# Layer 0's second and third late modulation burst: moved behind the scores of each half, their transposes laid out with the next burst's first step

## The chip, the cores and the metric

One core of one Trainium2 chip. The metric is the device time of one launch in microseconds (us). TensorE (PE) multiplies, VectorE (DVE), ScalarE (ACT) and GpSimd (POOL) work on SBUF and PSUM, and SyncE (SP) issues nearly all loads. Each engine works through its own list of instructions in order.

## The reference

Two layers (DEPTH 2) on one sequence, SEQ = D_MODEL = 1024, all in float32. What matters here, cut down:

```python
cond = jax.nn.silu(c)
for l in range(DEPTH):
    mod = (cond @ w_ada[l] + b_ada[l])[:, None, :]
    shift_a, scale_a, gate_a, shift_f, scale_f, gate_f = jnp.split(mod, N_MOD, axis=-1)
    h = rms_norm(x) * (1.0 + scale_a) + shift_a
    mix = hybrid_mixer(h, ...)          # gated linear attention (GLA) | latent attention (MLA)
    x = x + gate_a * mix
    h = rms_norm(x) * (1.0 + scale_f) + shift_f
    x = x + gate_f * (jnp.square(jax.nn.relu(h @ w_mlp_up[l])) @ w_mlp_down[l])
```

The six vectors of `mod` are numbered m = 0 to 5 in this order. So m = 2 (gate_a) is wanted after the mixer, and m = 3 and 4 (shift_f, scale_f) by the norm in front of the MLP. In the mixer, `h @ w_in` gives GLA's q, k (256 columns each), v, output gate g (512 each) and a decay input, and MLA's latents. GLA's scores inside a chunk are q k^T weighted with products of decays.

## The kernel before

**Matmuls.** A product is three fp32r matmuls on hi/lo splits of both operands (`mm3`: lines 161, 162, 163). A weight unit is loaded by SP (line 292, 512 KB), rounded to its high part on ACT or DVE (line 307) and its low part is the rest, made on POOL or DVE (line 308). 51 arena slots of 128x1024 hold all tiles; a slot that is freed is given to the next `AR.alloc()`, and its new load waits until the old tile's last reader is done. A name such as `s_141_1081` is slot counter and tile number.

**Order.** The list `PROGRAM` says in which order the mixer's code is written out; a scheduler then lays the instructions of all engines out by a simulated time line, with the order of the code as the priority. Halves A and B are the two halves of the 1024 tokens. The tokens that matter: `v` values and `g` gates of a half (weights as the moving operand, output token by token into four PSUM banks), `L` the latents with the decay input, `T` the rest of the latents (norms, decays `lg`, transposes), `Q` GLA's queries and keys, `W` GLA's scores, `O` GLA's output, `u` and `a` heads and attention of MLA, `H` the second half of the normed input.

**Scores (`gla_scores`, token W).** Score blocks are built level by level, H = 1, 2, 4, ..., 64, eight passes of score matmuls in all (line 912; one pass is eight instructions, which the profile counts as 16). For each level ACT makes exponentials of decays (lines 949, 955), DVE differences and sums of them (956, 961), POOL scales keys and queries (950, 927, 958), and the products come out of `ps_g` by DVE (938, 966, 973). Two tiles each for keys and queries alternate, which POOL clears first (902, 903). Then the keys are scaled and transposed (990, 998, 999), and `gla_out` multiplies (1038, 1042, 1048) and transposes its result (1068).

**Modulation bursts (`ada_steps`).** One vector m takes eight loads of 128x1024 of w_ada (line 245, 512 KB each), eight DVE steps that sum them with the condition as the scalar (line 254, then seven of line 256), eight PE transposes (line 263) and two DVE sums over the 128 partial columns (266, 267, and 269 for m = 1 and 4). In layer 0, m = 0 and 1 are made at the start, m = 2, 3, 4 by the tokens X2, X3, X4 in the mixer, m = 5 and layer 1's six vectors step by step inside the MLP of layer 0 (`ADA_ORDER`, `UP_ADA`, `DOWN_ADA`).

## Time and profile before

| | |
|---|---|
| time, three runs | 2334.77 us median (2326.91 to 2339.45) |
| the profiled execution | 2329.49 us, of it 2327.7 us span |
| PE busy | 2228.0 us, 96% of the span |
| DVE busy | 1785.4 us, 77% |
| ACT busy | 1137.8 us, 49% |
| POOL busy | 457.3 us, 20% |
| w_ada loads of 512 KB | 80, 5.1 us from issue to landing |

PE is at work nearly all the time, so what counts are the few places where it is not. The stages that the change touches lie between 50 and 365 us of the span. Busy time of matmuls is modelled at their ends, so starts are the better measure of PE's pace.

### The profile page before, as it was taken

The page shows a single profiled execution, that of the slowest core. Times are in us where ns is not written, and L with a number is a line of the kernel's source. Part 1 is how long each engine was busy: PE and PEld are TensorE (multiplying, and loading weights), DVE is VectorE, ACT ScalarE, POOL GpSimd, SP SyncE. Part 2 cuts the span into 40 slices and gives each one's busy share as a digit, 9 for nine tenths or more (in the row PEclk, how much of TensorE's full clock was granted, in tenths as well). Part 3 has the DMA queues.
Part 4 walks back from the last instruction along what each step waited for, and adds up shares of the span by engine and source line. Part 5 has one row for each costly group of instructions (what it writes and reads, how often), then busy time and mean ns, then how long its engine had stood idle before and what let it go on. Part 6 is the DMA issues. An engine that isn't in the chain of part 4 may idle for free.

```text
span 2327.7 us, 29242 instructions
## 1 busy us (share of the span) xinstructions
PE 2228.0 (96%) x11016; PEld 1851.0 (80%) x11016; DVE 1785.4 (77%) x2453; ACT 1137.8 (49%) x1764; POOL 457.3 (20%) x326
## 2 busy tenths in 40 slices
PE   7989999999999999998999999999999999999999
PEld 4778788888788877886888888887888888887887
DVE  5987769757989788889996756986665867887794
ACT  3464647535632483433535555665365228633341
POOL 2544533410030000000074345342002000000000
PEclk9999999999999999999999999999999999999999
DMA  9632210236678655765741221004354564365562
GB/s 345 202 105 81 82 30 1 82 106 221 207 220 276 192 163 200 243 229 193 241 138 34 63 61 41 10 10 125 130 160 138 184 196 145 113 231 195 166 208 82
DMA packets 236657, 340.41 MB, mean 146 GB/s; under 512 B 11078, under 2 KB 150500, under 8 KB 236516
## 3 DMA queue, kind: packets, MB, share of 16 engines
q1 hardware_dynamic: 235968, 338.08, 44.8%
q8 instruction: 86, 1.41, 0.3%
q14 instruction: 55, 0.45, 0.1%
q10 hardware_dynamic: 548, 0.48, 0.1%
HBM read 317.54 MB, written 20.97 MB: 145 GB/s over the span
## 4 chain that ended last, share of the span: by engine, by line
PE 66%; DVE 14%; DMA 7%; ACT 2%; issue 2%; POOL 1%; SPq 0%; DVEq 0%; ACTq 0%; POOLq 0%
PE ps_m L162 9%; PE ps_m L163 9%; PE ps_m L161 8%; PE ps_s L162 6%; PE ps_s L163 6%; PE ps_s L161 6%; PE ps_g L163 4%; PE ps_g L162 4%; PE ps_g L161 4%; DMA s<-in_w_mlp_down_dram 3%; PE ps_x L163 2%; PE ps_x L162 2%; DMA s<-in_w_ada_dram 2%; PE ps_x L161 2%; DMA s<-in_w_mlp_up_dram 2%
## 5 line engine op out<-in xcount | busy, mean ns | idle before, releaser
L307 ACT CAST s<-s 128x1024 fp32r<-128x1024 f32 (+2 forms) x306 | 314.8, 1035 | 474.1 <-DVE s L304 243.2
L162 PE MATMUL ps_m<-s,s 128*128 128x512 f32 (+2 forms) x1212 | 462.2, 382 | 15.4 <-DVE s L1273 15.4
L161 PE MATMUL ps_m<-s,s 128*128 128x512 f32 (+2 forms) x1212 | 460.4, 383 | 10.4 <-ACT s L1272 3.9
L163 PE MATMUL ps_m<-s,s 128*128 128x512 f32 (+2 forms) x1212 | 459.1, 379 | 1.6 <-DVE s L308 1.5
L308 POOL TENSOR_TENSOR s<-s,s 128x1024 fp32r<-128x1024 f32 (+2 forms) x90 | 229.2, 2558 | 1051.6 <-ACT s L307 696.5
L161 PE MATMUL ps_s<-s,s 128*128 128x512 f32 (+5 forms) x928 | 356.9, 388 | 9.0 <-ACT s L719 3.1
L163 PE MATMUL ps_s<-s,s 128*128 128x512 f32 (+5 forms) x928 | 354.6, 384 | 1.8 <-DVE s L308 1.3
L162 PE MATMUL ps_s<-s,s 128*128 128x512 f32 (+5 forms) x928 | 354.7, 383 | 0.0
L308 DVE TENSOR_TENSOR s<-s,s 128x1024 fp32r<-128x1024 f32 x224 | 270.0, 1217 | 55.8 <-ACT s L307 45.6
L304 DVE TENSOR_TENSOR s<-s,s 128x1024 f32<-128x1024 f32 x160 | 198.4, 1242 | 119.0 <-DMA s<-in_w_mlp_up_dram 81.7
L162 PEld LDWEIGHTS ps_m<-s,s 128*128 128x128 f32 x1212 | 230.4, 190 | 59.1 <-DVE s L1273 18.5
L161 PEld LDWEIGHTS ps_m<-s,s 128*128 128x128 f32 x1212 | 229.3, 189 | 54.9 <-ACT s L1272 6.1
L163 PEld LDWEIGHTS ps_m<-s,s 128*128 128x128 f32 x1212 | 230.0, 190 | 42.7 <-DVE s L308 2.5
L1272 ACT CAST s<-s 128x1024 fp32r<-128x1024 f32 x140 | 146.7, 1050 | 187.6 <-DVE s L1270 57.3
L161 PEld LDWEIGHTS ps_s<-s,s 128*128 128x128 f32 x928 | 174.7, 188 | 47.2 <-ACT s L719 6.1
L163 PEld LDWEIGHTS ps_s<-s,s 128*128 128x128 f32 x928 | 175.2, 189 | 37.8 <-issue 3.0
L162 PEld LDWEIGHTS ps_s<-s,s 128*128 128x128 f32 x928 | 175.4, 189 | 32.8 <-issue 1.5
L162 PE MATMUL ps_g<-s,s 128*128 128x512 f32 (+1 forms) x506 | 195.2, 387 | 0.7 <-DVE s L1273 0.7
L161 PE MATMUL ps_g<-s,s 128*128 128x512 f32 (+1 forms) x506 | 194.6, 388 | 0.0
L163 PE MATMUL ps_g<-s,s 128*128 128x512 f32 (+1 forms) x506 | 194.4, 387 | 0.1
L1273 DVE TENSOR_TENSOR s<-s,s 128x1024 fp32r<-128x1024 f32 x140 | 173.6, 1244 | 14.9 <-ACT s L1272 11.1
L162 PE MATMUL ps_x<-s,s 128*128 128x512 f32 (+3 forms) x362 | 124.2, 344 | 1.5 <-DVE s L743 1.5
(320 smaller groups left out, 3636.1 us busy)
## 6 DMA issues: line engine op xcount, KB each, us to landing
s<-in_w_mlp_up_dram SPq DMA_DIRECT2D x192, 512.0 KB, 4.8
s<-in_w_mlp_down_dram SPq DMA_DIRECT2D x192, 512.0 KB, 4.3
s<-in_w_ada_dram SPq DMA_DIRECT2D x80, 512.0 KB, 5.1
s<-in_w_in_dram SPq DMA_DIRECT2D x48, 512.0 KB, 3.8
s<-in_w_ada_dram SPq DMA_DIRECT2D x32, 256.0 KB, 4.1
xd<-s SPq DMA_DIRECT2D x16, 512.0 KB, 4.5
s<-in_w_out_dram SPq DMA_DIRECT2D x16, 512.0 KB, 4.3
s<-xd SPq DMA_DIRECT2D x16, 512.0 KB, 3.4
```

Source lines behind the costliest of these rows:

```text
L161: PE.matmul(o, lh, rh, start=start, stop=False)
L162: PE.matmul(o, lh, rl, start=False, stop=False)
L163: PE.matmul(o, ll, rh, start=False, stop=stop)
L304: V.tensor_tensor(raw[:, :n], raw[:, :n], u.second[:, :n], op=ALU.add if u.sign > 0 else ALU.subtract)
L307: (V.tensor_copy if u.eng[-2] == "v" else S.copy)(R(u.hi[:, :n]), raw[:, :n])
L308: (V if u.eng[-1] == "v" else G).tensor_tensor(R(u.lo[:, :n]), raw[:, :n], u.hi[:, :n], op=ALU.subtract)
L1272: S.copy(R(hi), t)
L1273: V.tensor_tensor(R(lo), t, hi, op=ALU.subtract)
```

## The change

In `PROGRAM`, X (m = 2) stays; the burst of m = 3 moves from ahead of `Hb WA` (scores of half A) to behind `TB`, ahead of `QB`; the burst of m = 4 moves from between `QB` and `WB` to behind `gB`, ahead of the first head. A burst is now taken from one generator for all three vectors, eight steps at a time: the eight loads and DVE steps are laid out by X, and the eight transposes and sums by the first step of the next X, and for the last vector by the new token Z behind `vB`. The bursts of the MLP hand their transposes on in the same way, and `DOWN_ADA` takes one step more at m = 2. Lines behind the edits have smaller numbers: 4 to 6 less up to line 590, 4 less from 591 to 1153 (L912 becomes L908, L961 L957, L256 L252).

```diff
--- before.py
+++ after.py
@@ -35,7 +35,7 @@
 
 
 PROGRAM = (
-    "vA E X2 R LA Ha =1 TA QA X3 Hb WA gA OA LB TB QB X4 WB gB u00 P1 vB u01 a00 P1 "
+    "vA E X R LA Ha =1 TA QA Hb WA gA OA LB TB X QB WB gB X u00 P1 vB Z u01 a00 P1 "
     "P1 a01 OB =2 F U1 a02 a03 a10 a12 a11 a13 U2 a20 a21 a22 U3 a23 M0 =3 a30 a31 F M1 a32 D0 D1 "
     "D2 =0 a33 F D3 D4 D5 F D6 D7 N "
 ).split()
@@ -57,7 +57,7 @@
 
 ADA_ORDER = ((0, 5), (1, 1), (1, 0), (1, 2), (1, 4), (1, 3), (1, 5))
 UP_ADA = {2: range(8), 4: range(8), 1: (2, 6), 7: (1, 3, 5, 7), 6: range(1, 7), 5: (1, 3, 5, 7), 3: range(1, 7)}
-DOWN_ADA = {m: range(1, 7) for m in (4, 5, 2)}
+DOWN_ADA = {4: range(1, 7), 5: range(1, 7), 2: range(7)}
 
 UP_ENGINES = {1: "vag"}
 TAGS = {
@@ -233,10 +233,6 @@
         k = l * 48 + m * 8 + d
         return mod[:, k:k + 1]
 
-    def ada(l, m):
-        for _ in ada_steps(l, m):
-            pass
-
     def ada_steps(l, m, tag=lambda: "x"):
         acc = AR.alloc()
 
@@ -255,8 +251,7 @@
             else:
                 V.scalar_tensor_tensor(acc, raw, cond[:, k:k + 1], acc, op0=ALU.mult, op1=ALU.add)
             AR.free(raw)
-            if k < 7:
-                yield
+            yield
         for hb in range(2):
             ps = bank(tag())
             for b in range(4):
@@ -268,7 +263,6 @@
             if m in (1, 4):
                 V.tensor_scalar(mod[:, k0:k0 + 4], mod[:, k0:k0 + 4], 1.0, None, op0=ALU.add)
         AR.free(acc)
-        yield
 
 
 
@@ -588,6 +582,8 @@
         G.tensor_tensor(m2[:, :, 32:64], src[:, :, 0:32], Sn[:, :, 32:64], op=ALU.mult)
         G.tensor_tensor(dst[:, :, 0, :], m1, m2, op=ALU.add)
         G.tensor_tensor(dst[:, :, 1, :], m1, m2, op=ALU.add)
+
+    ada_work0 = (None for m in (2, 3, 4) for _ in ada_steps(0, m))
 
 
     wg = cp.tile([32, 256], F32, name="wg")
@@ -1151,9 +1147,10 @@
                 flush()
             elif kind == "=":
                 tags = TAGS[rest]
-            elif kind == "X":
+            elif kind in "XZ":
                 if l == 0:
-                    ada(0, int(rest))
+                    for _ in range(8 if kind == "X" else 1):
+                        next(ada_work0, None)
             elif kind == "P":
                 ahead(ustate["pos"] + int(rest))
             elif kind == "D":
@@ -1323,7 +1320,7 @@
                     if left[b] == 0 and b != (0, 1):
                         square_relu(C[b][g])
                 if l == 0 and g in UP_ADA[m]:
-                    next(ada_work)
+                    next(ada_work, None)
             for hi, lo in moving:
                 AR.free(hi, lo)
             moving = moving_next
@@ -1390,7 +1387,7 @@
                 AR.free(hi, lo)
                 drop(u)
                 if l == 0 and g in DOWN_ADA.get(m, ()):
-                    next(ada_work)
+                    next(ada_work, None)
             for q in range(4):
                 for (r, c), sign in PRODUCTS[m][2]:
                     d = r * 4 + q
```

**PE, the end of the gates of half A.** The first fence is before, from the gates' last product on; in names such as `s19_159_1151` the first number is the slot, tiles 156 to 159 are the keys and queries of the levels, and a pass is two rows, one for each PSUM bank.

```order
L161 MATMUL ps_s_1336<-s15_168_1339,s32_74_410 128x512
L162 MATMUL ps_s_1336<-s16_169_1340,s32_74_410 128x512
L163 MATMUL ps_s_1336<-s15_168_1339,s32_74_410 128x512
L263 MATMUL ps_x_1106<-cs_81,s34_141_1081 128x128 x4
L263 MATMUL ps_x_1114<-cs_81,s34_141_1081 128x128 x4
L912 MATMUL ps_g_1177<-s19_159_1151,s47_156_1148 128x128 x4
L912 MATMUL ps_g_1183<-s19_159_1151,s47_156_1148 128x128 x4
L912 MATMUL ps_g_1197<-s18_158_1150,s24_157_1149 128x128 x4
L912 MATMUL ps_g_1203<-s18_158_1150,s24_157_1149 128x128 x4
```

Five more passes of two rows each follow there, and then the eight key transposes (L998). Now, from the gates' last product to the first output product (the levels' tiles are 147 to 150):

```order
L908 MATMUL ps_g_1180<-s40_149_1093,s33_148_1092 128x128 x4
L908 MATMUL ps_g_1186<-s40_149_1093,s33_148_1092 128x128 x4
L163 MATMUL ps_s_1279<-s16_159_1282,s32_74_410 128x512
L908 MATMUL ps_g_1200<-s9_150_1094,s41_147_1091 128x128 x4
L908 MATMUL ps_g_1206<-s9_150_1094,s41_147_1091 128x128 x4
L908 MATMUL ps_g_1220<-s40_149_1093,s33_148_1092 128x128 x4
L908 MATMUL ps_g_1226<-s40_149_1093,s33_148_1092 128x128 x4
L908 MATMUL ps_g_1240<-s9_150_1094,s41_147_1091 128x128 x4
L908 MATMUL ps_g_1246<-s9_150_1094,s41_147_1091 128x128 x4
L994 MATMUL ps_g_1262<-cs_81,s28_128_936 128x128 x4
L994 MATMUL ps_g_1268<-cs_81,s28_128_936 128x128 x4
L1038 MATMUL ps_g_1430<-s44_80_428,s50_145_1089 128x128 x4
```

Seven score passes stood behind the gates, with the transposes of m = 3 ahead of them; now three do, five stand among the gates' products, the transposes are gone, and output products have come forward.

**DVE, ahead of the scores of half A.** Before, behind the latents' norm (L961 and L956 are the first decay steps, on the tile `s_119`):

```order
L451 SCALAR_TENSOR_TENSOR s_124_931<-ps_x,colsv,s_124_931 128x512
L872 TENSOR_TENSOR s_126_948<-ps_x,s_126_948 128x512
L254 TENSOR_SCALAR s_141_1081<-s_142_1082,cond 128x1024
L256 SCALAR_TENSOR_TENSOR s_141_1081<-s_143_1084,cond,s_141_1081 128x1024
L256 SCALAR_TENSOR_TENSOR s_141_1081<-s_144_1087,cond,s_141_1081 128x1024
L256 SCALAR_TENSOR_TENSOR s_141_1081<-s_145_1090,cond,s_141_1081 128x1024
L256 SCALAR_TENSOR_TENSOR s_141_1081<-s_146_1093,cond,s_141_1081 128x1024
L256 SCALAR_TENSOR_TENSOR s_141_1081<-s_147_1096,cond,s_141_1081 128x1024
L961 TENSOR_TENSOR s_119_866<-s_119_866 128x512
L256 SCALAR_TENSOR_TENSOR s_141_1081<-s_148_1099,cond,s_141_1081 128x1024
L956 TENSOR_TENSOR s_161_1156<-s_119_866 128x512
L961 TENSOR_TENSOR s_119_866<-s_119_866 128x256x2
L256 SCALAR_TENSOR_TENSOR s_141_1081<-s_149_1102,cond,s_141_1081 128x1024
```

Now, from the line that makes the decays (L828, before L832) on:

```order
L828 SCALAR_TENSOR_TENSOR s_119_850<-ps_x,tmp 128x512 x2
L424 SCALAR_TENSOR_TENSOR tmp<-s_13_160,mod,s_4_123 128x512
L424 SCALAR_TENSOR_TENSOR tmp<-s_14_167,mod,s_4_123 128x512
L424 SCALAR_TENSOR_TENSOR tmp<-s_15_174,mod,s_4_123 128x512
L957 TENSOR_TENSOR s_119_850<-s_119_850 128x512
L952 TENSOR_TENSOR s_152_1099<-s_119_850 128x512
L445 SCALAR_TENSOR_TENSOR s_122_899<-ps_x,colsv,s_122_899 128x512
L957 TENSOR_TENSOR s_119_850<-s_119_850 128x256x2
L424 SCALAR_TENSOR_TENSOR tmp<-s_16_181,mod,s_4_123 128x512
L445 SCALAR_TENSOR_TENSOR s_123_907<-ps_x,colsv,s_123_907 128x512
L957 TENSOR_TENSOR s_119_850<-s_119_850 128x128x4
L426 SCALAR_TENSOR_TENSOR s_144_1080<-tmp,mod,s_144_1080 128x512
```

The eight steps of the burst are gone from here, and the first decay step stands ahead of the latents' norm (L445, before L451).

**DVE, behind the scores of half B.** Before, from the copies of the transposed keys (L999) to the first head's norm factors (L396); L645 empties a value bank:

```order
L999 COPY s_236_2190<-ps_g 128x512 x2
L655 TENSOR_REDUCE ssq<-s_253_2388 128x4
L645 TENSOR_TENSOR s_254_2389<-ps_s,s_254_2389 128x256
L645 TENSOR_TENSOR s_254_2389<-ps_x,s_254_2389 128x256
L651 TENSOR_REDUCE ssq<-s_255_2411 128x4
L652 TENSOR_REDUCE ssq<-s_255_2411 128x4
L391 TENSOR_SCALAR rs_v<-ssq 128x8
L391 TENSOR_SCALAR rs_v<-ssq 128x4
L394 SCALAR_TENSOR_TENSOR rs_a<-rs_y 128x12
L395 TENSOR_TENSOR rs_a<-rs_a,rs_v 128x12
L396 SCALAR_TENSOR_TENSOR rst<-rs_a,rs_y 128x12
```

Now:

```order
L995 COPY s_227_2131<-ps_g 128x512
L250 TENSOR_SCALAR s_242_2315<-s_243_2316,cond 128x1024
L995 COPY s_227_2131<-ps_g 128x512
L252 SCALAR_TENSOR_TENSOR s_242_2315<-s_244_2318,cond,s_242_2315 128x1024
L252 SCALAR_TENSOR_TENSOR s_242_2315<-s_245_2321,cond,s_242_2315 128x1024
L641 TENSOR_TENSOR s_254_2371<-ps_s,s_254_2371 128x256
L641 TENSOR_TENSOR s_254_2371<-ps_x,s_254_2371 128x256
L252 SCALAR_TENSOR_TENSOR s_242_2315<-s_246_2324,cond,s_242_2315 128x1024
L651 TENSOR_REDUCE ssq<-s_253_2370 128x4
L252 SCALAR_TENSOR_TENSOR s_242_2315<-s_247_2327,cond,s_242_2315 128x1024
L385 TENSOR_SCALAR rs_v<-ssq 128x8
L252 SCALAR_TENSOR_TENSOR s_242_2315<-s_248_2330,cond,s_242_2315 128x1024
```

The burst of m = 4 now lies between the key copies and the norm of the first head, three of its steps ahead of L641 (before L645).

## Rows read from the trace of the kernel before

**Rows 1.** The page: busy us of each engine; the chain that ended last, by engine.

```profile
PE 2228.0 (96%) x11016; PEld 1851.0 (80%) x11016; DVE 1785.4 (77%) x2453; ACT 1137.8 (49%) x1764; POOL 457.3 (20%) x326
...
PE 66%; DVE 14%; DMA 7%; ACT 2%; issue 2%; POOL 1%; SPq 0%; DVEq 0%; ACTq 0%; POOLq 0%
```

**Rows 2.** Stretches: length, busy (x) of PE, PEld, DVE, ACT, POOL; PEclk, DMA, GB/s.

```profile
146.60:174.00 27.40, 18.41 (x105) 16.48 (x104) 27.31 (x38) 22.41 (x38) 12.75 (x9) 0.81 0.20 59
...
246.00:283.00 37.00, 32.35 (x224) 28.65 (x222) 29.16 (x41) 28.54 (x49) 22.61 (x14) 1.00 0.25 74
283.00:310.00 27.00, 26.69 (x127) 22.23 (x125) 10.81 (x17) 7.51 (x15) 14.74 (x12) 0.94 0.10 29
```

**Rows 3.** PE's timeline, end of the scores of half A: start, length, instruction, wait.

```profile
102.73 1.98 PE L827 MATMUL ps_x<-s,wg 17*128 17x512 f32 x4 [2.15 <-DVE s L823]
...
143.86 1.03 PE L263 MATMUL ps_x<-cs,s 128*128 128x128 f32 x8
144.73 1.95 PE L912 MATMUL ps_g<-s,s 128*128 128x128 f32 x16
150.36 3.40 PE L912 MATMUL ps_g<-s,s 128*128 128x128 f32 x16 [3.69 <-DVE s L966]
...
157.29 6.79 PE L912 MATMUL ps_g<-s,s 128*128 128x128 f32 x32 [1.10 <-DVE s L973]
...
171.38 1.16 PE L912 MATMUL ps_g<-s,s 128*128 128x128 f32 x8 [0.52 <-DVE s L973]
...
174.07 0.48 PE L161 MATMUL ps_m<-s,s 128*128 128x464 f32 x1 [0.21 <-ACT s L307]
```

**Rows 4.** PE's timeline, second half: mm3 pace, key transposes, first output products.

```profile
241.12 0.39 PE L161 MATMUL ps_s<-s,s 128*128 128x512 f32 x1
...
247.01 0.39 PE L163 MATMUL ps_s<-s,s 128*128 128x512 f32 x1
...
282.06 1.10 PE L998 MATMUL ps_g<-cs,s 128*128 128x128 f32 x8 [2.17 <-DVE s L990]
283.48 2.07 PE L1038 MATMUL ps_g<-s,s 128*128 128x256 f32 x4 [0.31 <-DVE s L999]
```

**Rows 5.** DVE's timeline ahead of the scores of half A.

```profile
114.43 0.68 DVE L832 SCALAR_TENSOR_TENSOR s<-ps_x,tmp 128x512 f32<-128x512 f32 x1
...
129.08 0.75 DVE L254 TENSOR_SCALAR s<-s,cond 128x1024 f32<-128x1024 f32 x1 [4.31 <-DMA s<-in_w_ada_dram]
129.87 6.57 DVE L256 SCALAR_TENSOR_TENSOR s<-s,cond,s 128x1024 f32<-128x1024 f32 x5
```

**Rows 6.** POOL's timeline, clearing of score tiles of half A.

```profile
130.04 0.96 POOL L903 MEMSET s<- 128x1024 f32 x1 [6.99 <-DVE s L254]
```

**Rows 7.** Line 256 over the whole span: min/median/max ns, first and last start.

```profile
L256 DVE SCALAR_TENSOR_TENSOR s<-s,cond,s x70: 1264/1283/3098, 62.2 to 1143.8; 128x1024 f32<-128x1024 f32 x70
```

**Rows 8.** Landing times of w_ada loads, 100 to 300 us.

```profile
DMA to landing us min/median/max: 3.9/5.6/5.7
```

**Rows 9.** DVE's timeline in the stretch of half B: first decay step, burst's last step.

```profile
224.48 1.26 DVE L961 TENSOR_TENSOR s<-s 128x512 f32<-128x512 f32 x1 [0.21 <-ACT s L949]
...
242.20 2.22 DVE L256 SCALAR_TENSOR_TENSOR s<-s,cond,s 128x1024 f32<-128x1024 f32 x1
```

**Rows 10.** DVE's timeline behind the scores of half B.

```profile
284.52 0.42 DVE L645 TENSOR_TENSOR s<-ps_s,s 128x256 fp32r<-128x256 f32 x1
```

**Rows 11.** POOL's timeline behind the scores of half B.

```profile
279.15 11.20 POOL L308 TENSOR_TENSOR s<-s,s 128x640 fp32r<-128x640 f32 x5 [3.27 <-ACT s L307]
290.67 1.12 POOL L660 TENSOR_TENSOR s<-s,rst 128x256 f32<-128x256 f32 x1 [0.31 <-DVE rst L396]
291.86 1.06 POOL L586 TENSOR_TENSOR s<-s,s 128x256 f32<-128x256 f32 x1
```

**Rows 12.** DVE's timeline, one operation twice (POOL's block of line 308 at 90 us).

```profile
87.22 0.29 DVE L545 TENSOR_SCALAR s<-s 128x256 f32<-128x256 f32 x1
...
93.36 2.38 DVE L545 TENSOR_SCALAR s<-s 128x256 f32<-128x256 f32 x1
```

## The prediction

> **What bounds the kernel now.** I first read the busy shares and the chain that ended last: TensorE (PE) is busy for 96% of the span, and the chain lies on it for 66% [rows 1]. So a change moves the time only where it makes PE wait, ends such a wait, or changes the granted clock. I then cut the stretch in which the bursts lie into pieces by stage [rows 2]. The reader is to see one poor piece among good ones: from 146.6 to 174.0 us PE is busy for 18.4 of 27.4 us at a mean granted clock of 0.81, while DVE is busy for 27.3. Two pieces behind it have 32.4 of 37.0 and 26.7 of 27.0 us.
>
> That piece is the end of the gated scores of the first half (token WA), and PE's own rows tell its story [rows 3]. The gates of half A and a first score pass behind them are through at 146.7. From 150.36 to 172.5 stand 96 score matmuls, that is six passes of 16 (the first and the last row are shown), then the eight key transposes of line 998, and at 174.07 the first matmul of LB. A pass that waits for nothing took 1.95 us; here one took 3.40 and two took 6.79, nearly each with a wait for the DVE evacuation of the pass before (line 973). Work in the piece: 6 × 1.95 + 1.1 (line 998's eight in the second half, [rows 4]) = 12.8 us. Lost: 27.4 − 12.8 = 14.6 us, partly wait and partly half clock.
>
> Why are the scores late? DVE's rows ahead of them [rows 5]: lg, which the decays need, is ready at 115.1, but DVE stands idle for 4.31 us until the first w_ada tile of burst m=3 lands, does L254 at 129.08 and five L256 in one block until 136.4. The first decay step, L961, comes behind that block. GpSimd's clearing of a score tile waited 6.99 us for L254 as well [rows 6], since that tile's slot had held what the burst reads.
>
> **A: scores of half A without a burst (the gain).** The change takes eight loads and eight DVE steps (0.75 + 7 × 1.28 = 9.7 us [rows 5, 7]) from in front of the scores. In the new DVE order L957 (before: L961) follows three norm steps behind L828 (L832), and the clears wait for no burst. So the chain of levels starts some 14 us earlier (about 115 + 7 for those steps and the other work around them, against 136). In the new PE order 40 of the 64 score instructions stand among the gates and 24 behind them; 8 and 56 it was before. Eight instructions are one pass (16 in the profile): three passes are left at the end instead of the first one and the six of the piece. I let each of these three cost 1.5 us more than its work (they still alternate with evacuation: six passes between 150.36 and 172.5 took 3.7 each, 1.7 more than 1.95). Lost then 4.5 instead of 14.6: −10.1. The eight transposes of burst m=3 inside this stretch (1.03, [rows 3]; started to start 0.8) leave it: −0.8. Ahead of it, the transposes and reductions of m=2 leave PE and DVE before L827, which waited 2.15 us for DVE [rows 3]: −2.0. Sum −12.9. Bounds: −17 if all 14.6 and the 2.8 go; −5 if five passes inside the gates wait 1.6 us each in PE's order.
>
> **B: LB to the scores of half B.** Burst m=3 now lies in this stretch, between the latent norm's L445 steps and the first decay step of half B. Its loads are queued on SP behind the loads of QB and before those of the last gate tiles; the first two of them reuse the gate slots of half A, which are free only after line 1068's transposes. A w_ada load of this stretch took 5.6 us to land (median, [rows 8]). The burst m=4 that stood here before goes; four of its eight steps stood ahead of the latent norm, and its last one came as late as 242.20 [rows 9]. So DVE's work is the same and its order different. By my count of the new order the burst ends about 8 us after QB's last matmul; the score pass at level H=2, the first whose decay comes wholly behind the burst, stands 22 us behind that point on PE, and its chain (decay, exponential, product, copy: some 7 us from its L961 at 224.5 on before, [rows 9]) leaves about 7 us in hand. Cover: the gates of half B, and PE idles 4.65 us from 246 to 283 already [rows 2]. I take 0, and +0.8 for the transposes of m=2, which now stand in QB (m=4's leave, m=3's come). Bounds −3 (some of the 4.65 goes, since no L256 is late any more) and +8 (burst as late again as it is now taken to be).
>
> **C: behind the scores of half B.** Burst m=4 comes here, beside vB, and three of its steps stand in DVE's order before L641 (L645), which frees the fourth bank vB needs. Let T be the end of the key transposes (283.2, [rows 4]). The third tile's load goes when their source's slot is free: T + 0.4 to issue + 5.6 + one L256 1.28 + 0.42 for L645 [rows 10] = T + 7.7. PE wants the bank after the output matmuls (T + 1.8) and 20 rows of vB at 0.227 each (26 of them from 241.12 to 247.01, [rows 4]): T + 6.3. A wait of about 1.4 us. Behind it five more L256 delay the norm of the first head (rst) from T + 7.4 [rows 11] to about T + 15.6 (7.7 + 5 × 1.28 + some 1.5 of small steps). On GpSimd, L656 (1.12 us) waits for it, and behind that stand a weight split, three rope products (1.06 and two of half that) and the split of vB's last unit; at 2.2 us a split (five in 11.20, [rows 11]), that unit is ready near T + 23. PE wants it after 76 matmuls and the head's two groups of transposes: T + 1.8 + 17.3 + 1.6 + 1.4 = T + 22. Another 1 to 2 us, and 0.8 for m=4's transposes (Z): +4. Bounds: 0 (the loads land in 3.9, the shortest, and vB covers) and +10 (each step delayed until its tile lands by itself).
>
> **The rest.** PE's order is the same again from about 365 us on but for small moves of layer 1's transposes by one MLP step; their count and work stay, and the loads of w_ada there run under matmuls. I take 0 ± 3.
>
> **Sum.** −12.9 + 0.8 + 4 + 0 = about −8 us, made against the profiled execution's 2329.49 (span 2327.7): 2321.5. That run lies below the median shown (2334.77); the four runs average 2332.6 and spread over 0.5%, which is also what a measurement of this kernel can tell from no change (11.7 us). From the average: 2332.6 − 8 = 2325.
>
> **Rivals.** *Nothing is given back:* B and C are hidden, −13 to −17, time about 2319. For it: the cover in [rows 2] from 283 to 310, PE 26.7 of 27.0. Against it: in that cover PE has no room for a late bank. *The scores wait inside the gates:* a pass now comes every 20 matmuls (4.5 us plus the pass), and levels on their own ran at 3.7, so the chain keeps up if it starts in time; if not, five passes wait 2 us each and only −3 is left, with C +4 about +1: 2334. *Slower: the burst in front of the scores again, now in B.* Its first tiles land late, DVE stands before L250 as it stood before L254, and the whole loss of A, 14.6 us, is paid in B: −12.9 + 0.8 + 14.6 + 4 = +6.5, about 2339. It decides from a burst that ends some 15 us behind QB instead of 8; the sum is then zero. For it: this is the very pattern of [rows 5]. Against it: six of the eight slots are free early, and only two loads can be late. *Contention of DVE and GpSimd:* the steps of m=4 now run beside a block of five splits on GpSimd [rows 11]. A DVE step of 0.29 us took 2.38 once beside splits on GpSimd [rows 12], and one L256 of 70 took 3.10 instead of 1.28 [rows 7]. If all seven do, rst comes 7 × 1.8 = 12.7 us later, of which some 2 are covered: about +10 in C more than counted, +2 in all, 2335.
>
> The Trainium skill, "SBUF — State Buffer", section "Who interferes with whom", speaks for this last case: a DVE instruction with two SBUF inputs contends with a GpSimd instruction that reads SBUF, and whichever issues first shuts the other out for its whole length. By it every L256 beside a split would wait for up to a split. The median of 1.28 among 70 says that most did not meet one or did not wait, and the 3.10 that it happens.
>
> **How the numbers follow.** Forecast (−13 to −3 net) 0.44; nothing given back 0.24; waits inside the gates 0.15; burst in front of scores B 0.11; contention 0.06. Faster by over 0.5% needs −11.7: nearly all of the second case (0.23) and the outer quarter of the first (0.12), 0.35. Slower by over 0.5%: only where the slower rival comes with C's bad bound or a late burst beyond it, 0.10. The rest, 0.55, is within 0.5%. The range reaches from 2310 (the lowest run shown less 17) to 2340 (the slower rival); the likeliest case's own is 2318 to 2331.
>
> **What would show it.** In lines of the changed program. Right for A: the time from the end of the last pass that runs beside the gates to the first 128x464 matmul of LB falls from 27.4 to about 13 us, its clock goes back towards 1.0, the clears and L957 wait for no w_ada, and score passes lie among the gates without waits. Wrong: waits of L908 for line 969 or a GpSimd product inside the gates. For B: idle PE no more than 5 us from QB to the key transposes, and L250 done before the gates; wrong if L957 of half B comes behind a wait for w_ada that PE then shares. For C: a PE wait of 1 to 2 us on L641, another on vB's last split, and L656 some 8 us later after the key transposes than now. The prediction fails as a whole if PE's waits before 365 us in all do not fall by 5 to 12 us, or if the MLP stages differ by more than 3.

## The result, and the profile after

The changed kernel takes 2351.93 us (median of six runs, 2345.80 to 2354.72) against 2333.31 for the kernel before (six runs): a ratio of 1.0079 [1.0057, 1.0100]. It is slower by 18.6 us, where 8 us of gain were forecast, and the time lies outside the range given (2310 to 2340). The profiled execution took 2351.24 us, span 2349.5.

The page after, busy time and the chain that ended last [rows 1]:

```profile
PE 2238.4 (95%) x11016; PEld 1858.4 (79%) x11016; DVE 1797.7 (77%) x2453; ACT 1139.2 (48%) x1764; POOL 455.0 (19%) x326
...
PE 69%; DVE 16%; DMA 7%; issue 3%; ACT 3%; POOL 1%; SPq 0%; DVEq 0%; ACTq 0%; POOLq 0%
```

The counts of instructions are the same. DVE has 12.3 us more of busy time for the same 2453 instructions: some of them got longer.

**Where the time went.** Both traces have 11016 matmuls in nearly the same order, so the start of the k-th can be compared with that of the k-th before. The table gives this difference for the matmul that started at 150, 200, ... us before, in us; plus is late. The kernels e1 to e13 are among the experiments below. In the column of 100 us the changed kernel, e1 and e12 seem 5 to 9 us late only because six matmuls fewer stand ahead of PE's wait in front of L823 (below): the count sets matmuls on either side of that wait against each other, and at 90 us these kernels are 1 to 4 us late.

```
                          100    150    200    250    300    450    550    850    900   1150   1250    end
after                     7.7   -1.0   -1.3    0.6    0.0    5.5    5.5    7.0   11.1   12.2   21.8   21.8
e1 mixer part only        5.3   -3.8   -3.6   -1.9   -2.1    0.6    0.6    2.1    0.7   -0.8   -0.7    0.3
e2 MLP part only          0.4    0.4    0.2    1.0   -0.4   -0.5   -0.5   -0.1    3.5    4.5   14.7   11.2
e3 moves, no hand-on      0.6   -4.7   -7.9   -8.3   -8.1   -4.6   -4.4   -4.4   -5.9   -7.4   -7.4   -7.0
e4 only m=3 moved         1.3   -3.5   -6.7   -6.1   -0.1    2.4    2.4    3.7    2.9    0.0    0.0   -4.2
e5 hand-on in UP          2.1    3.5    3.3    5.7    4.1    6.6    6.6    5.2    7.6    4.9    4.9    3.6
e7 hand-on in DOWN, g=7   1.2    3.4    3.7    4.1    2.7    5.2    5.2    7.6    6.5    9.6    8.5    7.2
e8 as e2, not (1, 1)      2.3    4.5    4.2    4.6    4.1    6.7    6.7    5.8    7.3   10.5   21.3   21.3
e9 step at g=0 only       0.9    0.7    0.5    0.2    0.3    1.4    1.8    3.4    2.1    0.7    9.3    7.7
e10 m=2 at once           1.0   -4.3   -7.5   -2.6    4.6    4.9    4.9    4.6    4.8    3.9    3.9    2.4
e11 bursts in project     1.4   -3.9   -7.0   -9.6  -10.6   -8.5   12.7   14.4   15.1   14.4   14.4   15.1
e12 change with g=7       9.3    0.1    0.0    2.9    2.6    5.0    5.0    5.3    8.6   10.8    9.7    5.7
e13 bursts spread         0.4   -4.9   -8.1  -10.6  -10.0   -7.9    0.6    2.0    2.9   -0.3    0.0   -0.1
```

In this trace the mixer ends 5.5 us late, not 8 early (e1, the same mixer, 0.6 late: single executions differ by that much, see the last section); 16 us more are lost in layer 0's MLP, most of them at about 865 and 1200 us. That is where the prediction had set 0 ± 3.

**The mixer.** The same stretches as in [rows 2], with one ahead of them, same columns:

```profile
103.00:146.60 43.60, 42.90 (x194) 33.82 (x195) 38.83 (x45) 25.61 (x43) 27.60 (x22) 0.88 0.13 37
146.60:174.00 27.40, 22.75 (x134) 19.29 (x134) 22.04 (x31) 19.50 (x33) 5.58 (x4) 0.94 0.26 77
246.00:283.00 37.00, 33.31 (x215) 29.84 (x216) 30.56 (x43) 25.54 (x45) 17.69 (x13) 0.95 0.33 104
283.00:310.00 27.00, 22.90 (x97) 18.24 (x96) 16.85 (x19) 9.07 (x17) 17.77 (x12) 0.94 0.24 70
```

PE's timeline after, L823 and the end of the scores of half A [rows 3]:

```profile
103.56 3.77 PE L823 MATMUL ps_x<-s,wg 17*128 17x512 f32 x4 [2.83 <-DVE s L819]
...
152.76 1.95 PE L908 MATMUL ps_g<-s,s 128*128 128x128 f32 x16
...
155.50 1.13 PE L908 MATMUL ps_g<-s,s 128*128 128x128 f32 x8 [0.56 <-DVE s L969]
157.87 3.14 PE L908 MATMUL ps_g<-s,s 128*128 128x128 f32 x24 [1.24 <-DVE s L969]
163.10 3.12 PE L908 MATMUL ps_g<-s,s 128*128 128x128 f32 x16 [2.08 <-DVE s L969]
...
170.87 0.48 PE L161 MATMUL ps_m<-s,s 128*128 128x464 f32 x1 [0.69 <-ACT s L301]
```

Passes lie among the gates without a wait, three are left behind them, and from the end of the last pass ahead of these (154.7) to LB it is 16.2 us instead of 27.4, some 3 us of it output products that now stand in front of LB; the clock of the stretch is 0.94 instead of 0.81. But LB begins only 3.2 us earlier (174.07 before). The piece in front of it had lost time in this trace: its clock is 0.88, where the kernel before had 0.96 in the same stretch (e1, with the same mixer, 0.96 too), and L823 still waits.

Behind that, PE's timeline after, scores of half B and vB [rows 4]:

```profile
246.21 3.65 PE L908 MATMUL ps_g<-s,s 128*128 128x128 f32 x16 [3.59 <-ACT s L951]
...
282.43 0.50 PE L162 MATMUL ps_m<-s,s 128*128 128x512 f32 x1 [1.01 <-POOL s L302]
...
287.99 0.50 PE L161 MATMUL ps_s<-s,s 128*128 128x512 f32 x1 [1.16 <-DVE s L641]
```

**The MLP.** PE's waits there, grouped by what it waited for (total, times, longest), 850 to 1282 us after:

```profile
PE ps_m L162 <- DVE s L1270: 14.2, 6, 4.7
PE ps_m L161 <- DVE s L1395: 7.6, 1, 7.6
PE ps_m L161 <- ACT s L1269: 7.4, 1, 7.4
```

And before, 840 to 1260 us:

```profile
PE ps_m L162 <- DVE s L1273: 10.5, 5, 4.5
PE ps_m L161 <- ACT s L1272: 3.9, 2, 3.2
...
PE ps_m L161 <- DVE s L1398: 0.9, 1, 0.9
```

One wait of 0.9 us became one of 7.6: the evacuation of the last down product (L1398, now L1395). One of 3.2 became 7.4: the first moving operand of the down products at the end of UP. The waits for low parts of moving operands (L1273, now L1270) grew by 3.7 us. The three make 14 of the 16 us.

### The profile page after: what moved, and what is told of

It is laid out like the page before. It is cut to its first block, busy times and chain, and to the rows that moved or that the text cites. A ratio compares the mean times of both kernels' runs of the same rounds, so it can differ in the third digit from the quotient of the medians.

```text
span 2349.5 us, 29219 instructions
## 1 busy us (share of the span) xinstructions
PE 2238.4 (95%) x11016; PEld 1858.4 (79%) x11016; DVE 1797.7 (77%) x2453; ACT 1139.2 (48%) x1764; POOL 455.0 (19%) x326
## 4 chain that ended last, share of the span: by engine, by line
PE 69%; DVE 16%; DMA 7%; issue 3%; ACT 3%; POOL 1%; SPq 0%; DVEq 0%; ACTq 0%; POOLq 0%
PE ps_m L162 9%; PE ps_m L163 9%; PE ps_m L161 9%; PE ps_s L162 6%; PE ps_s L163 6%; PE ps_s L161 6%; PE ps_g L163 4%; PE ps_g L161 4%; PE ps_g L162 4%; DMA s<-in_w_ada_dram 3%; PE ps_x L162 2%; PE ps_x L163 2%; PE ps_x L161 2%; DMA s<-in_w_mlp_up_dram 2%; DMA s<-in_w_mlp_down_dram 2%
## 5 line engine op out<-in xcount | busy, mean ns | idle before, releaser
L161 PE MATMUL ps_m<-s,s 128*128 128x512 f32 (+2 forms) x1212 | 462.8, 385 | 21.4 <-DVE s L1395 7.6
L1270 DVE TENSOR_TENSOR s<-s,s 128x1024 fp32r<-128x1024 f32 x140 | 171.3, 1229 | 13.0 <-ACT s L1269 10.1
```

The costliest lines, as they stand in the source:

```text
L161: PE.matmul(o, lh, rh, start=start, stop=False)
L1270: V.tensor_tensor(R(lo), t, hi, op=ALU.subtract)
```

## The experiments

Two theories stood at the start: (1) the loss is made in the MLP by the hand-on there and is independent of the mixer; (2) it is carried over from the mixer, whose end the MLP's schedule follows.

**e1 and e2: each half of the change by itself.** e1 has the moved bursts and the hand-on in the mixer, with the MLP as before; e2 the reverse:

```diff
-DOWN_ADA = {m: range(1, 7) for m in (4, 5, 2)}
+DOWN_ADA = {4: range(1, 7), 5: range(1, 7), 2: range(7)}
...
-    def ada_steps(l, m, tag=lambda: "x"):
+    def ada_steps(l, m, tag=lambda: "x", late=False):
...
-            if k < 7:
+            if late or k < 7:
                 yield
...
-        yield
+        if not late:
+            yield
```

> The mixer part of the change alone: bursts moved and their transposes handed on in layer 0's mixer, the MLP's bursts as before. Theory 1 (two separate losses: the trace after shows PE 5.5 us late at 450 us of the span and 21.8 us at its end, so 16 us are lost in the MLP by the handing-on there): 5 us over before, ratio about 1.002, PE late by 3 to 7 us from 450 us on to the end. Theory 2 (the MLP's loss is only carried over from the mixer, by the order of slots and by late starts): 18 to 22 us over before, ratio about 1.008, and PE falls back by 16 us more behind 600 us although nothing is changed there.

> The MLP part alone: layer 1's bursts and m=5 hand their transposes on, DOWN_ADA with one step more, the mixer as before. Theory 1: 16 us over before, ratio about 1.007, PE level with before up to 600 us, then late by some 4 us at the end of the last UP product (870 us) and by 7 us at 1200 us. Theory 2: no more than 2 us over before, ratio 1.000, and no wait at 870 us longer than the 3.6 us of before.

e1: 1.0014 [0.9999, 1.0028]. e2: 1.0079 [1.0063, 1.0095], the whole loss. Theory 2 falls: e2's mixer is the old one, and its PE is on time until 850 us. The 18 us are the MLP part's; the mixer part costs 3 us by e1's ratio, which its interval does not tell from nothing.

**e3 and e4: the moves without the hand-on.** e3 writes X3 behind TB and X4 behind gB, each summed at once; e4 moves only X3.

```diff
-    "vA E X2 R LA Ha =1 TA QA X3 Hb WA gA OA LB TB QB X4 WB gB u00 P1 vB u01 a00 P1 "
+    "vA E X2 R LA Ha =1 TA QA Hb WA gA OA LB TB X3 QB WB gB X4 u00 P1 vB u01 a00 P1 "
```

> Both bursts moved in the mixer, but each with its own transposes at once, as in the kernel before; the MLP as before. If handing the transposes on is what costs in the mixer (m=2's sums gone from ahead of L827, the wait there then 2.8 us with a longer time at half clock, worth some 5 us): the time before L827 as in before (wait 2.1), PE late by 0 or early by up to 5 us at 450 us, ratio 0.998 to 1.000. If the places cost: PE late by 4 to 6 us at 450 us as in the changed kernel, ratio 1.002. Theory 2 of the MLP would add its 16 us to either.

> Only the burst of m=3 moved (behind TB), with its transposes at once; m=4 stays ahead of the scores of half B, the MLP as before. By the trace after, the scores of half A give back 8 us, of which 4 go again in a wait ahead of the scores of half B: PE early by 3 to 6 us at 280 us and no wait of 3 us at 301 us, since m=4 isn't behind the scores; ratio 0.997 to 0.999. If m=3 is what makes the scores of half B wait, two bursts there make it worse: PE level with before or late by up to 6 us at 260 us, ratio 1.000 to 1.003.

e3: 0.9988 [0.9976, 0.9999]; e4: 1.0005 [0.9994, 1.0015]. Both are 7 to 8 us early at 200 us, where e1 and the change itself are 3.6 and 1.3. The gain in front of LB is real, but 7 to 8 us against this trace of the kernel before and not 12.9. (Nine traces have the mixer of before; at 200 us the other eight are 0.1 to 4.2 us late, the mean of the nine is 2.0. Against that mean the six kernels with m = 2 summed at once, e3, e4, e10, e11, e13 and e14, gain some 9 us there, and the three that hand it on, the change, e1 and e12, some 4.) e4 has lost all of it again at 300 us, e3 loses 3.5 between 300 and 450.

**e10: m = 2 summed at once, the rest of the mixer part as changed.**

```diff
-    ada_work0 = (None for m in (2, 3, 4) for _ in ada_steps(0, m))
+    ada_work0 = (None for m in (2, 3, 4) for _ in ada_steps(0, m, late=m > 2))
```

> The mixer part with m=2's transposes and sums at once again (its place is as in before), m=3 and 4 handing on as in the change, the MLP as before. If the missing sums of m=2 change DVE's order ahead of the decay matmuls (L827 in the kernel before) so that PE waits there and falls to the half clock for 9 us: PE level with before at 110 to 120 us (under 1.5 us late, 5 in the mixer part), early by 4 to 8 us at 200 us, ratio 0.998 to 1.000. If the handing-on of m=3 and m=4 costs instead: ratio as in the mixer part, 1.001 to 1.002.

1.0019 [1.0006, 1.0032], and 7.5 us early at 200 us instead of e1's 3.6: handing on m = 2 costs half of the gain there. One part shows in DVE's timeline after. With the sums gone, the rope table's steps stand earlier in its list, and three that take 0.42 us alone took 5.63 beside GpSimd's splits; L819, which L823 waits for, is behind them:

```profile
89.89 5.63 DVE L542 SCALAR_TENSOR_TENSOR s<-s 128x256 f32<-128x256 f32 x3
...
102.50 0.97 DVE L819 COPY s<-ps_x 16x512 f32<-16x512 f32 x1
```

That part is small: L823 waits 2.83 us with m = 2 handed on and 2.16 in e10, 0.7 more, and rope steps meet splits in the kernel before as well [rows 12]. By the table e1 and e10 stand nearly alike at 150 us (−3.8, −4.3). The same comparison puts them at −7.2 and −7.6 at 165 us and at −4.4 and −7.8 at 174, so they part where LB begins; what holds PE there stays open. And e10 is no faster than e1 over the whole: in and behind the scores of half B it loses 12 us (−7.5 at 200, +4.6 at 300). The medians do not reward the 4 us.

**e5, e6, e7, e8, e9, e12: which part of the MLP's edit.** e5 hands on only the first four bursts (those in UP), e6 only the last three and has the step at g = 0, e7 is e6 with that step at g = 7, e8 is e2 without the hand-on of (1, 1), e9 is the kernel before with the step at g = 0 alone, and e12 is the whole change with g = 7. Their edits are e2's but for the condition that picks the bursts (e5's is shown) and the range:

```diff
-    ada_work = (None for w in ADA_ORDER for _ in ada_steps(*w, lambda: other_tag[0]))
+    ada_work = (None for w in ADA_ORDER for _ in ada_steps(*w, lambda: other_tag[0], w in ADA_ORDER[:4]))
...
-DOWN_ADA = {4: range(1, 7), 5: range(1, 7), 2: range(7)}
+DOWN_ADA = {4: range(1, 7), 5: range(1, 7), 2: range(1, 8)}
```

> The MLP part again with the mixer as before, but only the first four bursts (m=5 of layer 0, m=1, 0, 2 of layer 1), which end in the up products, hand their transposes on; the last three and DOWN_ADA as before. If the two losses seen in the MLP part alone (PE late by 3.6 us at 865 us, by 11 more up to 1250 us) come each from the bursts of its own stage: 3 to 5 us over before, ratio 1.001 to 1.002, wait at 865 us over 7 us, and no more than 2 us are added at 1200 us. If the later loss is the earlier one's echo (DVE late at 865 us stays late): the whole 12 to 15 us, ratio about 1.006.

> Only the last three bursts (m=4, 3, 5 of layer 1), which end in the down products, hand their transposes on, with the additional step at g=0 of m=2's product as in the change; the first four as before. Each stage its own: nothing lost at 865 us, 8 to 12 us lost at 1050 to 1250 us, ratio 1.004 to 1.005. Echo: nothing lost anywhere, ratio 1.000.

> As the run before, but the additional step stands at the last group (g=7) of m=2's product and not at the first. If the additional step at g=0, which puts two more loads and a DVE step into the start of that product, makes the loss at 1200 us: under 4 us over before, ratio 1.000 to 1.002. If handing on itself makes it, by other slots and another order of DVE, or if the last sums now stand in front of the norm of layer 1: 8 to 14 us, ratio 1.003 to 1.006.

> The whole MLP part, except that the burst of m=1 of layer 1 sums its columns in its own last step (group 7 of the second product) and doesn't hand them on into the third product, the only one whose splits are on GpSimd; there the two small additions of 1.0 took 2.46 us together beside a split instead of 0.16 each. If that contention makes the loss at the end of the up products: PE level with before at 900 us (late by under 1.5 us), and 8 to 12 us lost later as in the whole part, ratio 1.004 to 1.006. If the loss at 865 us comes from the other bursts' sums (1.6 us of DVE work moved a step later): late by 3 us or more at 900 us and ratio 1.006 to 1.008.

> The kernel before with nothing but the additional step at g=0 of m=2's down product (DOWN_ADA), no burst handing anything on, so that the last burst's steps come one group earlier and the 57th call finds nothing. If that place alone makes the wait at 1200 us (9.5 us there in the runs that have the step, none in the one that has it at g=7): 6 to 10 us over before, ratio 1.003 to 1.004, a wait of 8 to 10 us for the evacuation at 1200 us. If it needs the handing-on as well: ratio 0.999 to 1.001 and a wait under 2 us there.

> The whole change with one number altered: the additional step of m=2's down product at the last group and not at the first. If the step at g=0 is 8 to 9 us of the change's 18: 9 to 11 us over before, ratio 1.0035 to 1.005, no wait over 2 us at 1210 to 1220 us. If the step only sets off what another delay would set off as well: ratio 1.006 to 1.009 as in the change.

| | ratio |
|---|---|
| e5, hand-on in UP | 1.0032 [1.0019, 1.0046] |
| e6, hand-on in DOWN with g = 0 | 1.0051 [1.0035, 1.0066] |
| e7, the same with g = 7 | 1.0014 [0.9999, 1.0028] |
| e8, all but (1, 1), with g = 0 | 1.0080 [1.0065, 1.0094] |
| e9, only the step at g = 0 | 1.0033 [1.0018, 1.0048] |
| e12, the whole change with g = 7 | 1.0030 [1.0014, 1.0045] |

The number in `DOWN_ADA` is as large a part as any: +0.33% alone (e9), 0.37% between e6 and e7, 0.49% between the change and e12. UP gives 0.32, g = 0 0.33, the hand-on in DOWN 0.14, and these add up to e2's 0.79, each known to about 0.15.

*What the step at g = 0 does.* In e9 PE waits 7.65 us for L1398, which stands in DVE's list behind layer 1's first norm (L414 to L432). DVE's timeline of the kernel before, from the norm's first step to the evacuation:

```profile
1178.06 0.68 DVE L414 TENSOR_SCALAR tmp<-ps_g 128x512 f32<-128x512 f32 x1
1180.16 0.79 DVE L417 SCALAR_TENSOR_TENSOR tmp<-tmp 128x512 f32<-128x512 f32 x1 [1.42 <-ACT tmp L416]
1180.99 0.69 DVE L418 TENSOR_TENSOR tmp<-tmp 128x512 f32<-128x512 f32 x1
...
1183.87 4.10 DVE L430 SCALAR_TENSOR_TENSOR tmp<-s,mod,tmp 128x512 f32<-128x512 f32 x3
...
1193.86 0.74 DVE L432 SCALAR_TENSOR_TENSOR s<-tmp,mod,s 128x512 fp32r<-128x512 f32 x1
...
1199.59 2.71 DVE L1398 SCALAR_TENSOR_TENSOR s<-ps_m,mod,s 128x512 f32<-128x512 f32 x4
```

GpSimd's splits in the kernel before:

```profile
1168.67 11.73 POOL L308 TENSOR_TENSOR s<-s,s 128x1024 fp32r<-128x1024 f32 x3 [490.46 <-ACT s L307]
1182.99 3.11 POOL L308 TENSOR_TENSOR s<-s,s 128x1024 fp32r<-128x1024 f32 x1 [2.58 <-DVE s L307]
1191.71 6.26 POOL L308 TENSOR_TENSOR s<-s,s 128x928 fp32r<-128x928 f32 x1 [5.62 <-ACT s L307]
```

The same instructions of DVE in e9, and GpSimd's blocks beside them:

```profile
1178.12 0.69 DVE L414 TENSOR_SCALAR tmp<-ps_g 128x512 f32<-128x512 f32 x1 [2.60 <-PE ps_g L412]
...
1181.14 2.34 DVE L417 SCALAR_TENSOR_TENSOR tmp<-tmp 128x512 f32<-128x512 f32 x1
1183.51 2.77 DVE L418 TENSOR_TENSOR tmp<-tmp 128x512 f32<-128x512 f32 x1
...
1187.04 2.08 DVE L430 SCALAR_TENSOR_TENSOR tmp<-s,mod,tmp 128x512 f32<-128x512 f32 x3
...
1191.02 2.68 DVE L432 SCALAR_TENSOR_TENSOR s<-tmp,mod,s 128x512 fp32r<-128x512 f32 x1
...
1207.31 2.72 DVE L1398 SCALAR_TENSOR_TENSOR s<-ps_m,mod,s 128x512 f32<-128x512 f32 x4
```

```profile
1170.43 15.29 POOL L308 TENSOR_TENSOR s<-s,s 128x1024 fp32r<-128x1024 f32 x4 [488.47 <-DVE s L307]
1190.82 4.94 POOL L308 TENSOR_TENSOR s<-s,s 128x928 fp32r<-128x928 f32 x2 [5.09 <-ACT s L307]
```

The norm starts at the same time and reaches the evacuation after 29.2 instead of 21.5 us, with the same instructions in nearly the same order: steps of 0.7 us take 2.3 to 2.8 beside GpSimd. Some 3 us of the difference come before the first L430, beside the block of four splits, of which three were through at 1180.4 in the kernel before. The other 4.6 come behind it: splits and rope products on GpSimd from 1190.8 to 1204.6 stand beside slow steps of DVE in e9, while in the kernel before DVE kept its pace to 1195.8 and the split at 1191.71 took 6.26 us. The busy time between these starts, first before, then in e9 (columns as in [rows 2]), shows it for DVE as a whole, 28.1 us for what took 19.9:

```profile
1178.06:1199.59 21.53, 21.53 (x97) 17.83 (x96) 19.94 (x27) 9.21 (x13) 13.33 (x5) 1.00 0.40 129
```

```profile
1178.12:1207.31 29.19, 23.09 (x102) 18.77 (x100) 28.09 (x26) 9.52 (x13) 21.43 (x12) 0.97 0.25 71
```

In e12 the norm starts earlier against PE (at 1182.23, 4.2 us later than before, when PE is some 10 us later). It takes 27.1 us even there, but PE does not wait for it, and behind its first steps it is GpSimd that is held up, two splits in 15.79 us:

```profile
1195.62 15.79 POOL L302 TENSOR_TENSOR s<-s,s 128x1024 fp32r<-128x1024 f32 x2 [3.17 <-DVE s L301]
```

These lengths come back from trace to trace. From the norm's first step to the evacuation it is 21.5 us in seven runs without the step at g = 0 (before, e1, e3, e4, e5, e10, e11), and PE waits 0.9 to 1.0 us at that place; in e13 it is 24.8 with a wait of 1.2, in e14 21.4 without one. It is 28.4 to 29.2 us in all five with it (the change, e2, e6, e8, e9), and PE waits 7.6 to 9.1. In e7 and e12, with the step at g = 7, it is 27.1, without a wait. So the contention makes the norm longer, and the place of the step also sets where the norm stands against PE.

**e15 and e16: the splits beside the norm off GpSimd.** e16 is the kernel before with the low parts of the four units of layer 1's first values made on DVE (and their high parts on ACT), e15 is e9 with the same edit:

```diff
-                    U[l, hf, kind, q] = add_unit(wi[:, q * 2:q * 2 + 2, c0:c0 + 512], 2, 512, "vg" if kind == "v" and hf == 0 else "ag")
+                    U[l, hf, kind, q] = add_unit(wi[:, q * 2:q * 2 + 2, c0:c0 + 512], 2, 512, ("vg", "av")[l] if kind == "v" and hf == 0 else "ag")
```

> The kernel before with the step at g = 0 alone (as e9), and the low parts of the four weight units of layer 1's first values made on DVE instead of GpSimd (their high parts on ACT instead of DVE), so that no block of four splits runs on GpSimd at 1170 to 1186 us beside layer 1's first norm. Theory (the 8 us are contention: the same DVE steps of the norm take 29 instead of 21 us beside GpSimd's splits): the norm's first steps take 0.7 to 0.8 us again, PE's wait for the evacuation of the m = 2 down product falls from 7.65 to under 2 us, ratio 0.999 to 1.001 and equal to that of the control e16. Rival (the evacuations are late because the step changes DVE's order or the norm's start): the wait of some 7 us stays, ratio about 1.003, 0.003 above e16.

> The control: the kernel before, with the low parts of the same four units on DVE and their high parts on ACT, and no step at g = 0. Both theories: no wait over 2 us for the evacuation of the m = 2 down product, ratio 0.999 to 1.001. If it is itself slower, the move of the splits costs something of its own, and e15 is to be compared with this run and not with the kernel before.

e15: 1.0032 [1.0018, 1.0046]; e16: 1.0026 [1.0013, 1.0039]. Without the block of four the step at g = 0 makes no difference that these runs tell (0.0006 apart), and PE's wait is the same in both, e15 first and e16 below it:

```profile
PE ps_m L161 <- DVE s L1398: 4.3, 1, 4.3
```

```profile
PE ps_m L161 <- DVE s L1398: 4.0, 1, 4.0
```

Both waits had been expected under 2 us and both ratios within 0.999 to 1.001. The edit costs 0.26% by itself, and e15 is no faster than e9 (1.0033). The norm's first steps are back at 0.7 us, but its later ones fall beside the next splits and the rope products on GpSimd, in e16 too, as its rows on DVE show:

```profile
1178.91 0.67 DVE L419 SCALAR_TENSOR_TENSOR tmp<-tmp 128x512 f32<-128x512 f32 x1
...
1186.72 2.22 DVE L432 SCALAR_TENSOR_TENSOR s<-tmp,mod,s 128x512 fp32r<-128x512 f32 x1 [1.04 <-ACT s L431]
```

In us, from DVE's and PE's rows:

| | first step to first L430 | from there to the evacuation | PE's wait |
|---|---|---|---|
| before | 5.8 | 15.7 | 0.9 |
| e9 | 8.9 | 20.3 | 7.6 |
| e15 | 6.5 | 20.1 | 4.3 |
| e16 | 6.2 | 20.8 | 4.0 |

So the runs show that 3.3 us of e9's wait need the block of four splits. The other 4.3 us are put down to the later splits and rope products by the rows alone: no run takes those off GpSimd, and the control has that loss without the step.

*What the hand-on in UP does.* The sums of burst (1, 1) now stand one step later, in product m = 1, the only one whose low parts are made on GpSimd. After the change, DVE's two small additions L264, 0.16 us each in the kernel before, and the first step of the next burst, 0.87 before:

```profile
667.86 2.27 DVE L250 TENSOR_SCALAR s<-s,cond 128x1024 f32<-128x1024 f32 x1 [1.70 <-DMA s<-in_w_ada_dram]
...
678.56 2.47 DVE L264 TENSOR_SCALAR mod<-mod 128x4 f32<-128x4 f32 x2
```

At the end of UP PE waits longer for the moving operand: 6.26 us in e5 and 7.43 after, 3.21 before. That DVE carries the lateness there is argued, and e8 tests it. e8, without (1, 1), has a start-to-start gap of 5.5 us there instead of e2's 7.6 (3.6 before): so (1, 1) is about half of that wait. But its ratio is no better than e2's. And of e5's 0.32% (7.5 us) its own trace shows only these 3. The rest of the hand-on's cost in the MLP stays open. The hand-on in DOWN shows in another wait: with it the waits for low parts of moving operands come to 11.9 to 14.2 us (the change, e2, e6, e7, e8, e12), in before, e5 and e9 to 8.0 to 10.5. The cause of this stays open too.

**e11, e13, e14: can the mixer's gain be kept?** e11 gives both bursts as lumps in the output projection (X3 behind D0, X4 behind D3). e13 spreads them there as single steps, two behind each D, and e14 only m = 4, one behind each D, with m = 3 behind TB as in e3:

```diff
-    "P1 a01 OB =2 F U1 a02 a03 a10 a12 a11 a13 U2 a20 a21 a22 U3 a23 M0 =3 a30 a31 F M1 a32 D0 D1 "
-    "D2 =0 a33 F D3 D4 D5 F D6 D7 N "
+    "P1 a01 OB =2 F U1 a02 a03 a10 a12 a11 a13 U2 a20 a21 a22 U3 a23 M0 =3 a30 a31 F M1 a32 D0 Y Y D1 Y Y "
+    "D2 Y Y =0 a33 F Y D3 Y Y D4 Y Y D5 F Y Y D6 Y Y D7 Y Y N "
...
+            elif kind == "Y":
+                if l == 0:
+                    next(ada_work0, None)
```

> Both bursts moved out of the scores altogether, into the output projection (m=3 behind D0, m=4 behind D3), where DVE is busy for 30 of 50 us and PE for all of it; transposes at once, the MLP as before. If the scores of both halves and the first heads are rid of the bursts and the projection hides them: 8 to 14 us under before, ratio 0.994 to 0.9965. If their loads delay those of the projection and the MLP, or the sums come too late for the norm: PE early by 8 us at 450 us and level or late at 600 us, ratio 0.998 to 1.003.

> Burst m=3 and m=4 are both taken out of the scores and given as 17 single steps, two behind each token D0 to D7 of the output projection; m=2 and the MLP are as before. The stretch up to 300 us is then that of the run with both bursts in the projection (10.6 us early). Theory (a burst costs what it stands in front of as a lump; as single steps it is hidden): PE is 8 to 10 us early at 450 us and still at 600 us, ratio 0.9955 to 0.997. Rival (the loads of w_ada delay those of w_out wherever they lie in the projection): 3 to 15 us lost again behind 450 us, ratio 0.999 to 1.005.

> Burst m=3 stands as a lump behind TB, as in the run with the moves alone; m=4 is given as nine single steps, one behind each token D0 to D7 of the output projection and one more. Theory (single steps are hidden): about 8 us early at 200 us, some 2 of it lost in the scores of half B, the rest kept to 600 us, ratio 0.996 to 0.998. Rival (the projection has no room for the loads): 3 us and more lost behind 450 us, ratio 0.999 to 1.003.

e11: 1.0052 [1.0034, 1.0069]; e13: 0.9990 [0.9978, 1.0002]; e14: 1.0007 [0.9992, 1.0022]. With no burst in the scores (e11, e13) PE is 10 us early at 250 to 300 us: so much is to be had there. It holds to 450 and is lost behind it, 21 us as lumps and 8.5 as single steps. The stretch from 440 to 460 us, before and in e13, columns as in [rows 2]:

```profile
440.00:460.00 20.00, 20.00 (x126) 18.05 (x125) 13.41 (x31) 11.50 (x29) 8.58 (x5) 0.92 0.44 134
```

```profile
440.00:460.00 20.00, 17.29 (x109) 14.79 (x108) 15.22 (x30) 7.17 (x17) 3.04 (x2) 1.00 0.96 313
```

The DMA engines are full there (0.96), and PE loses 2.7 us. In e11 PE waits 6.9 us at 500 us for the high part of a weight unit (L307). The rival of e13 holds in size, 8.5 us lost behind 450; whether the loads or DVE's 17 steps do it in e13 was not separated. The best version found is e3, at 0.9988, hardly told from no change.

## Why the prediction was wrong

- **The rest, "I take 0 ± 3", is the step that failed.** The order showed the same count and work in the MLP, and that was right. But the term left out what the new places of the steps do to DVE's order and to the work beside it on GpSimd. The hand-on and the added step cost 0.79% (e2), 18 us, four tenths of it from the one number in `DOWN_ADA` (e9). That number stood in the diff and had no line in the sum. For the four tenths the rows show a norm that became 7.7 us longer and a wait of 7.6 us behind it; for the four tenths of the hand-on in UP a longer wait at its end shows 3 of 7.5 us, and the rest stays open. By the text's own marks, the MLP stages differ by far more than 3 us, and PE's waits before 365 us did not fall by 5 to 12 us: they are 37.6 us before and 38.7 after.
- **Contention was a rival, with 0.06, but in the wrong place.** It was weighed in C alone, where DVE's burst steps meet five splits. It showed at 1178 to 1207 us, in a norm that the diff does not touch; e15 and e16 show that part of the loss there needs GpSimd's block of splits. The trace of the kernel before could have warned of it: of the 70 steps of L256 [rows 7] three took 2.2 to 3.1 us, and two of these lie in the MLP, at 634 and 664 us, beside splits on GpSimd. The Trainium skill, "SBUF — State Buffer", section "Who interferes with whom", has the rule that fits: whoever issues first holds the shared ports for its whole instruction, and issue order decides who blocks. The rows agree from both sides: DVE steps of 0.7 us at 2.3 to 2.8 in e9, GpSimd's two splits at 15.79 us in e12.
- **A, −12.9, had the right mechanism and the wrong size.** Passes went among the gates, the clears and decays of half A wait for no burst, and the tail fell to 16.2 us (about 13 forecast; the output products in it were not counted). It measures −6 to −8 us (e3, e4, e10, e11, e13, e14 at 200 us), some −9 against the mean of the nine traces with the old mixer, and 0 to −4 with m = 2 handed on. The −2.0 for L823 did not come: it waits 2.83 us instead of 2.15. So what A had wrong was the hand-on of m = 2, counted as a gain of 2 us: it cost some 5.
- **B, +0.8, was near.** The rival that put the whole 14.6 us there did not happen: one wait of 3.6 us for the first pass, and +1.9 us on PE between 200 and 250 us (e1: +1.7).
- **C, +4, came with its waits where they were put.** 1.16 us for L641 (1.4 forecast), 1.0 for a split on GpSimd, L656 some 10 us later behind the key transposes than before (8 forecast), and a mixer that loses 5.5 us from 300 to 450 after, 2.7 in e1, 3.5 in e3.
- **The mixer part alone** is 1.0014 [0.9999, 1.0028] (e1), against a forecast of 0.9966 (−8 of 2332.6): this too is refuted. A given its measured size with m = 2 handed on, −4, and +0.8 and +4 for B and C make about +1, which the interval holds.

## What to carry to other kernels

An edit that leaves counts and work alone may still shift DVE steps into a block of GpSimd work: read from the order which long DVE chain (here a norm with evacuations queued behind it) then lies beside splits, and price its steps by the slow rows of the trace, not by the median. Taking the splits off GpSimd was no cure here: the norm fell beside the next ones (e15, e16). Price every number in a table that the diff touches, however small, with an experiment of its own. And a gain on one stretch is worth only what the next stretch with a shared limit lets through: e13 carried 8 us for 250 us of the span and lost them where the DMA engines were full.

## What was not expected of the hardware

- Eight kernels with the order of the kernel before in the mixer (e2, e5, e6, e7, e8, e9, e15, e16) differ from it in their profiled executions by −1.3 to +6.7 us at 550 us. One execution's trace carries that much chance, so a mixer term of 5 us can't be read from one trace alone.
- The same wait in front of L823 left PE at half clock for different times. After the change the granted clock was 0.50 from 105 to 110 us and 0.69 from 110 to 115; in e1, with the same mixer, 0.66 and 1.00, as in the kernel before.
- Work of 128x4 elements can be dear: two additions of 0.16 us each took 2.47 us beside a split on GpSimd (678.51 to 680.93 us after).
